# Other prices in the list scheduler of a two-block transformer kernel

## The chip, the cores and the metric

One Trainium2 chip, one of its cores. The time is the device time of one execution in microseconds (us). The kernel before ran three times: 1303.06, 1300.27 and 1302.47 us, median 1302.47. The page and the rows below come from one further look with the hardware profiler.

## The reference

A float32 network on 256 tokens of width 1024, in two blocks; every product has to come out at float32 accuracy. Cut to what matters:

```python
# block 1
h = rmsnorm(x, attn_norm); proj = h @ w_in
o_a = mla_attention(...); o_b = moba_attention(...)          # 8 heads each
x = x + (sigmoid(gate_a) * (o_a @ w_o_mla) + sigmoid(gate_b) * (o_b @ w_o_moba)) @ w_out
x = x + hierarchical_moe(rmsnorm(x, ffn_norm), ...)          # 4 groups of 8 experts, top 2
x = rmsnorm(x, final_norm)
# one expert:  (silu(xb @ w_g[e]) * (xb @ w_u[e])) @ w_d[e]
# block 2, layers l = 0 and 1
x = x + even_mixer(rmsnorm(x), ...)   # l = 0: gated convolution and differential attention
x = x + odd_mixer(rmsnorm(x), ...)    # l = 1: stick-breaking attention
x = x + mem_attention(rmsnorm(x), rmsnorm(mem), ...)
x = x + conv_ffn(rmsnorm(x), w_up, w_conv, w_down)
```

## The kernel before

The activations stay on chip, features on the 128 partitions, the 256 tokens along them. Weights stream in as slabs of 1 MB (128 x 2048 floats), each one DMA of the queue of SyncE (SP). A float32 product is made of three fast ones: a slab `w` is split by ScalarE (ACT) into a rounded part `h` and by VectorE (DVE) into the rest `l`; the activations likewise into `xh` and `xl`; TensorE (PE) then adds xh by h, xl by h and xh by l. In the trace these are the groups of six or so matmuls named `fm` (output by features) and `tm` (output by tokens).

The 32 experts are computed in eight groups of four, g = 0 to 7, each expert on its first 32 tokens. The names of one group, in the order of its data: `ga` gathers the tokens with the selection matrix `st`, which is made from `place`, the token's place in line, itself made from the product `pos`; `cb`, `cs`, `rs` bring the norm factors and the weights of the tokens, from `ct` and `rt`; `gu` are eight products with raw slabs `w_gu`; `act` is the activation, `at` its transposition; `by` are four products with raw slabs `w_dn`, in two banks; `y` copies a bank of `by`; `co` scatters `y` back, and the residual `x` takes it. Expert slabs are used as they are, without `h` and `l`; between the groups steps of the memory's keys and values (slabs `w_xkv`, products `fm` and `tm`, norms `hn_raw`, `hn_sq`, `rsq`, `hn`) are mixed in.

Behind group 1 (LATEG) stands a branch, L1137: tokens that did not fit are computed if there are any, which with these inputs there are not. All engines read a flag and branch. SyncE first waits until its loads have landed.

Nothing of this is issued in the order of the code. The class `Recorder` records every operation with its inputs and outputs; `plan` then plays a list scheduler: each engine has a clock, of the operations that are ready on it the one of the lowest place in the program goes first, its clock moves on by `price`, and what depends on it becomes ready LAG later. Loads keep the order of the program and start as places come free. A place is one buffer of a tag: `w`, `h` and `l` have three each, `n8` six, and a raw expert slab takes a place of whichever of these tags can spare one. When the plan says a place is free depends on the prices, so they also decide which load gets which place, and so for whose last reader it waits. The order that `plan` gives is then issued (`issue`, whose line L461 nearly every instruction shows) and the tile framework adds the semaphores: on the chip each engine runs its list in order, whatever things really take. `barrier` keeps all but loads on their side of the branch.

Of the kernel before, what the change touches and what calls it, by code (L numbers as in the profile page):

```python
# [63 lines left out]
# Each engine runs its instructions in the order in which they are issued. The  # L64
# network is first recorded, phase after phase, on tiles that have no place yet;
# a list scheduler then picks the order, so that an engine that would wait for
# one phase works on the next. Tile places the tiles and makes all waits.
class View:
    """A part of a recorded tile."""
# [54 lines left out]
class Slot:  # L124
    """A recorded tile."""
# [38 lines left out]
class Recorder:  # L164
# [18 lines left out]
    def stray(self, shape, dtype, name):  # L183
        """A tile that takes a place that any of the tags in self.shared can spare."""
        return Slot(self, shape, dtype, name, None, 0, "sb").view()
# [5 lines left out]
    def price(self, engine, method, a, k):  # L191
        n = self.size(a[0])
        if engine == "tensor":
            if method == "transpose":
                return n / 1.2 + 3
            lhs, rhs = a[1], a[2]
            if rhs.dtype == F32R:
                return max(n / 2.4 + 3, 109) if n >= 254 else 213
            if rhs.dtype == BF16:
                return n / 2.4 + 3  # L200
            cost = max(4 * n / 2.4, 400 if n <= 64 else 213) + 3
            m, rows = self.size(lhs), lhs.rows() if isinstance(lhs, View) else lhs.shape[0]
            if m <= 32:
                return cost / 3.5
            return cost / 2 if m <= 64 or rows <= 64 else cost
        if engine == "scalar":
            return 100 + n / 1.2 + (90 if isinstance(k.get("scale"), (View, bass.AP)) else 0) \
                + (90 if "accum_out" in k else 0)
        if engine == "vector":
            src = a[1]  # L210
            if method in ("tensor_copy", "tensor_scalar"):
                psum = isinstance(src, View) and src.tile.space == "ps"
                return 70 + n * (1.04 if psum else 0.52)
            if method == "reciprocal":
                return 70 + 6.4 * n
            if method == "tensor_reduce":
                return 70 + 1.04 * self.size(src)
            return 70 + 1.04 * n + (60 if method == "scalar_tensor_tensor" else 0)
        if engine == "gpsimd":
            return 200 + 3.5 * n  # L220
        return 2915.0 * n / 2048 if engine == "sync" else 100

    def record(self, engine, calls):
# [18 lines left out]
        if engine == "sync":  # L242
            op.lag = 2000.0
# [39 lines left out]
    def barrier(self, fn, views):  # L283
        """All that was recorded before comes before fn(), all that follows after it, except loads."""
# [5 lines left out]
    def plan(self):  # L290
        """An order of everything recorded: on each engine the ready operation of the lowest prio goes first."""
# [17 lines left out]
        def spare(op):  # L309
            """The shared tag that can best spare a place for op: those of earlier ops stay."""  # L310
# [11 lines left out]
        def load():  # L322
            """Start the loads in the order of the program, as far as there are places."""
# [20 lines left out]
        def offer(op):  # L344
            """Hand a free place to each tile that op starts, in the order of the program, if there are."""
# [88 lines left out]
    def run(self):  # L434
# [7 lines left out]
        # a table is loaded as soon as the one before has done its last  # L442
# [21 lines left out]
class Net:  # L464
# [11 lines left out]
    def bank(self, tag, name):  # L476
        """A bank of PSUM: g for products with weights, a and b for chains in turn, m for the rest."""
        return self.rec.tile([128, 512], F32, name, "p" + tag, dict(g=3, a=2, b=2, m=1)[tag], "ps")

    def temp(self, p, name, shape, dt=F32):  # L480
        """A short-lived tile of chain p, or of the norms (p = "s")."""
# [51 lines left out]
    def raw(self, ap):  # L533
        """A slab of weights as it is."""
# [4 lines left out]
    def slab(self, ap, inner, before=None):  # L539
        """A slab of weights in two parts that add up to it exactly, each [128, n / inner, inner].  # L540
        With before, it comes in four pieces, and before(i) comes before piece i."""
# [1142 lines left out]
```

## Time and profile before

| | |
|---|---|
| median of three runs | 1302.47 us (1300.27 to 1303.06) |
| profiled execution, its span | 1302.4 us |
| TensorE, weight loads | 1234.3 us (95%), 1091.3 us (84%) |
| VectorE, ScalarE | 852.8 us (65%), 651.8 us (50%) |
| loads of SyncE's queue | 272.03 MB, 56.1% of 16 DMA engines |
| TensorE's mean granted clock | 0.987 |

The profiled execution is its span; the page gives no other time of it. By stage: block 1's attention to about 235 us, experts 235 to 525, even mixer to about 625, memory attention and first feed-forward to about 900, odd mixer to about 1050, memory attention and second feed-forward to the end. The share of an engine is a mean over these stages; the windows by stretch say more. A busy TensorE need not be at its peak, since the ends of matmuls are modelled.

### The profile page before, as it was taken

The numbers are of one execution on the slowest core, as the hardware profiler recorded it, in microseconds if no ns is written. First come the engines' busy times: TensorE is split into PE (matmuls) and PEld (weight loads), VectorE is DVE, ScalarE is ACT, GpSimd is POOL, SyncE is SP. The second block draws the span as 40 slices with busy tenths as digits, with TensorE's granted clock in tenths as the row PEclk, the third lists the DMA queues.
The fourth block names the chain that finished last, engine by engine and source line by source line (L and its number), as shares of the span: only waits on it lengthen the run. The fifth ranks groups of instructions, "written<-read, shape, count | busy, mean of one in ns | idle before, by whom it ended". The sixth has DMA issues, their size and how long they took to land.

```text
span 1302.4 us, 22667 instructions
## 1 busy us (share of the span) xinstructions
PE 1234.3 (95%) x9325; PEld 1091.3 (84%) x9325; DVE 852.8 (65%) x1529; ACT 651.8 (50%) x1111; POOL 8.9 (1%) x71
## 2 busy tenths in 40 slices
PE   7999999987878876999999999999999999999998
PEld 7988999656545542898999999999998999999997
DVE  7666578524442242898877977777745587877775
ACT  6654455423322231664545655555656655555553
POOL 1000000000000000000000000000000000000000
PEclk9999999998989998999999999999999999999999
DMA  7623375798999989353441555555333251555551
GB/s 257 241 98 130 136 285 204 309 393 333 381 379 396 419 335 406 133 191 123 156 175 66 198 196 186 170 191 193 131 130 114 81 194 66 203 185 189 174 188 65
DMA packets 40143, 273.55 MB, mean 210 GB/s; under 512 B 4576, under 2 KB 4576, under 8 KB 8032
## 3 DMA queue, kind: packets, MB, share of 16 engines
q1 hardware_dynamic: 40032, 272.03, 56.1%
q8 instruction: 75, 1.23, 0.4%
q14 instruction: 36, 0.29, 0.1%
HBM read 270.96 MB, written 1.05 MB: 209 GB/s over the span
## 4 chain that ended last, share of the span: by engine, by line
PE 67%; DVE 4%; DMA 2%; ACT 2%; issue 1%; SPq 0%; DVEq 0%; ACTq 0%
PE fm L461 40%; PE dn L461 10%; PE tm L461 4%; PE gu L461 2%; PE co L461 2%; PE oz L461 2%; DMA w<-w_dn 2%; DVE l L461 2%; PE by L461 2%; PE bo L461 1%; PE mo L461 1%; PE ms L461 1%; PE ga L461 1%; PE hn L461 1%; DMA w<-w_gu 1%
## 5 line engine op out<-in xcount | busy, mean ns | idle before, releaser
L461 PE MATMUL fm<-xh,h 128*128 128x256 f32 x1824 | 529.0, 291 | 14.1 <-ACT h L461 6.6
L461 PE MATMUL fm<-xh,l 128*128 128x256 f32 x1824 | 520.1, 286 | 6.7 <-DVE l L461 6.7
L461 PE MATMUL fm<-xl,h 128*128 128x256 f32 x1824 | 518.5, 285 | 0.0
L461 DVE TENSOR_TENSOR l<-w,h 128x1024 fp32r<-128x1024 f32 (+2 forms) x328 | 383.1, 1191 | 59.9 <-ACT h L461 59.2
L461 ACT ACTIVATE h<-w 128x1024 fp32r<-128x1024 f32 (+2 forms) x328 | 325.4, 1027 | 176.3 <-issue 85.1
L461 PEld LDWEIGHTS fm<-xh,h 128*128 128x128 f32 x1824 | 352.0, 193 | 19.2 <-ACT h L461 7.4
L461 PEld LDWEIGHTS fm<-xh,l 128*128 128x128 f32 x1824 | 352.0, 193 | 8.3 <-DVE l L461 8.0
L461 PEld LDWEIGHTS fm<-xl,h 128*128 128x128 f32 x1824 | 352.4, 193 | 2.1 <-issue 0.7
L461 PE MATMUL tm<-l,xh 128*128 128x256 f32 (+2 forms) x364 | 104.5, 288 | 4.0 <-DVE l L461 4.0
L461 PE MATMUL tm<-h,xh 128*128 128x256 f32 (+2 forms) x364 | 107.2, 296 | 0.1
L461 PE MATMUL tm<-h,xl 128*128 128x256 f32 (+2 forms) x364 | 104.0, 286 | 0.0
L461 DVE SCALAR_TENSOR_TENSOR fc<-fu,partile,fc 128x256 f32<-128x256 f32 x176 | 73.5, 480 | 1.3 <-ACT fc L461 1.3
L461 PEld LDWEIGHTS tm<-l,xh 128*128 128x128 f32 x364 | 69.5, 191 | 5.2 <-DVE l L461 4.6
L461 PEld LDWEIGHTS tm<-h,xh 128*128 128x128 f32 x364 | 69.4, 191 | 3.3 <-issue 1.6
L461 PE MATMUL gu<-w,xs 128*32 128x512 f32 x512 | 65.6, 630 | 6.0 <-DMA w<-w_gu 6.0
L461 PEld LDWEIGHTS tm<-h,xl 128*128 128x128 f32 x364 | 69.5, 191 | 0.4
L461 PE MATMUL dn<-fa,h 128*128 128x256 f32 x352 | 64.2, 282 | 1.1 <-ACT fa L461 0.6
L461 DVE TENSOR_TENSOR x<-x,co 128x512 f32<-128x512 f32 x32 | 21.8, 687 | 57.9 <-PE co L461 57.9
L461 PE MATMUL dn<-h,fa 128*128 128x512 f32 x176 | 57.0, 396 | 0.0
L461 PEld LDWEIGHTS dn<-fa,h 128*128 128x128 f32 x352 | 54.4, 189 | 1.6 <-ACT fa L461 0.8
L461 DVE TENSOR_TENSOR fu<-fm,rbc 128x512 f32<-128x512 f32 x44 | 30.3, 688 | 37.9 <-PE fm L461 37.7
L461 DVE SCALAR_TENSOR_TENSOR act<-gu,rs,act 128x256 f32<-128x256 f32 x8 | 3.9, 484 | 71.8 <-ACT act L461 71.8
(291 smaller groups left out, 1416.1 us busy)
## 6 DMA issues: line engine op xcount, KB each, us to landing
w<-w_gu SPq DMA_DIRECT2D x64, 1024.0 KB, 9.3
w<-w_up SPq DMA_DIRECT2D x44, 1024.0 KB, 4.9
w<-w_dn SPq DMA_DIRECT2D x32, 1024.0 KB, 9.9
w<-w_down SPq DMA_DIRECT2D x22, 1024.0 KB, 4.9
w<-w_xkv SPq DMA_DIRECT2D x16, 1024.0 KB, 8.5
w<-w_in_d SPq DMA_DIRECT2D x8, 1024.0 KB, 4.8
w<-w_xq SPq DMA_DIRECT2D x8, 1024.0 KB, 4.9
w<-w_xo SPq DMA_DIRECT2D x8, 1024.0 KB, 5.1
```

The costliest lines, as they stand in the source:

```text
L461: getattr(getattr(self.nc, op.engine), method)(*map(r, a), **{n: r(v) for n, v in k.items()})
```

## The change

Only the numbers of `price`, and one lag, are others. Where the formulas were the author's, they now follow the durations of a trace: a DMA of a slab 2485 instead of 2915 ns, ready 2400 instead of 2000 later; ScalarE's fixed part 205 instead of 100, VectorE's some 155 instead of 70; a fast matmul of 256 columns 120 instead of 110; transpositions and the slow float32 products by other formulas. Comments and doc strings are gone as well, and an empty line in `price` moves what follows by one line, so L461 is L462 after.

```diff
             if method == "transpose":
-                return n / 1.2 + 3
+                return 109 * max(1.0, n / 128)
             if rhs.dtype == F32R:
-                return max(n / 2.4 + 3, 109) if n >= 254 else 213
+                return max(n / 2.4 + 13.3, 109) if n >= 254 else 213
...
-            cost = max(4 * n / 2.4, 400 if n <= 64 else 213) + 3
+            cost = max(4 * n / 2.4 + 5, 218)
...
         if engine == "scalar":
-            return 100 + n / 1.2 + (90 if isinstance(k.get("scale"), (View, bass.AP)) else 0) \
-                + (90 if "accum_out" in k else 0)
+            return 205 + n / 1.2 + (77 if isinstance(k.get("scale"), (View, bass.AP)) else 0) \
+                + (204 if "accum_out" in k else 0)
...
-                return 70 + n * (1.04 if psum else 0.52)
+                return 155 + n * (1.04 if psum else 0.55)
...
-            return 70 + 1.04 * n + (60 if method == "scalar_tensor_tensor" else 0)
+            return 157 + 1.04 * n + (57 if method == "scalar_tensor_tensor" else 0)
...
-        return 2915.0 * n / 2048 if engine == "sync" else 100
+        return 2485.0 * n / 2048 if engine == "sync" else 100
...
         if engine == "sync":
-            op.lag = 2000.0
+            op.lag = 2400.0
```

Three quarters of TensorE's calls keep their place in its list (the largest move is 120 places), two thirds of VectorE's, 72% of ScalarE's and 257 of SyncE's 278. 26 of the loads get another place: among them the first `w_xkv` slab behind group 2's expert slabs, which had the place that the sixth `gu` of group 2 reads last and now has the second's; the second of these slabs behind group 4's, which had the place of the first `by` and now has that of the last `gu`; and the first `w_gu` slab for group 7, which had a place that frees with `co` and now one that frees with a split `l`.

At the branch, VectorE. What stands ahead of it before, from group 1's activation on:

```order
L461 SCALAR_TENSOR_TENSOR act<-gu,rs,act 128x256
L461 COPY act<-at 128x256
L461 TENSOR_TENSOR x<-x,co 128x512 x4
L461 TENSOR_TENSOR l<-w,h 128x1024 x2
L1127 TENSOR_LOAD flag
L1137 COMPARE_AND_BRANCH
```

And after:

```order
L462 SCALAR_TENSOR_TENSOR act<-gu,rs,act 128x256
L462 COPY act<-at 128x256
L462 TENSOR_TENSOR x<-x,co 128x512 x4
L1128 TENSOR_LOAD flag
L1138 COMPARE_AND_BRANCH
```

The two splits `l` that stood ahead of the branch are gone from there; the same holds on TensorE for 21 `fm`, and on ScalarE for four `h`. What stands on VectorE directly behind the branch (the slow part between, not run, left out), before:

```order
L461 TENSOR_TENSOR hn_raw<-fm,rbm 128x512
L461 TENSOR_TENSOR l<-w,h 128x1024 x2
L461 TENSOR_TENSOR hn_sq<-hn_sq 128x256
L461 TENSOR_TENSOR st<-place,csttile 128x256 x2
L461 TENSOR_TENSOR rsq_t<-rsq_u 128x256
L461 SCALAR_TENSOR_TENSOR rsq_t<-hn,rsq_t 128x256
```

And after:

```order
L462 TENSOR_TENSOR l<-w,h 128x1024 x4
L462 TENSOR_TENSOR hn_raw<-fm,rbm 128x512
L462 TENSOR_TENSOR hn_sq<-hn_sq 128x256
L462 TENSOR_TENSOR st<-place,csttile 128x256 x2
L462 TENSOR_TENSOR rsq_t<-rsq_u 128x256
L462 SCALAR_TENSOR_TENSOR rsq_t<-hn,rsq_t 128x256
```

All four splits are behind the branch now, and all four ahead of `hn_raw`, where before the last two came behind it.

In group 3, TensorE, from the first four `gu` to `co`; four calls make one product with a raw slab. Before:

```order
L461 MATMUL gu<-w,xs 32x512 x16
L461 MATMUL hn<-hn_sq,ones 128x256
L461 MATMUL gu<-w,xs 32x512 x4
L461 MATMUL cb<-csttile,ct 128x128
L461 MATMUL gu<-w,xs 32x512 x4
L461 MATMUL cb<-csttile,ct 128x128 x3
L461 MATMUL rs<-ones,rt 128x1 x4
L461 MATMUL gu<-w,xs 32x512 x8
L461 MATMUL at<-csttile,act 128x128 x2
L461 MATMUL by_6731<-w,act 32x512 x4
L461 MATMUL by_6736<-w,act 32x512 x4
```

And after:

```order
L462 MATMUL gu<-w,xs 32x512 x16
L462 MATMUL hn<-hn_sq,ones 128x256
L462 MATMUL gu<-w,xs 32x512 x16
L462 MATMUL at<-csttile,act 128x128 x2
L462 MATMUL cb<-csttile,ct 128x128
L462 MATMUL by_6721<-w,act 32x512 x4
L462 MATMUL cb<-csttile,ct 128x128 x3
L462 MATMUL rs<-ones,rt 128x1 x4
L462 MATMUL by_6732<-w,act 32x512 x4
L462 MATMUL by_6721<-w,act 32x512 x4
L462 MATMUL co<-cs,y 128x256 x4
```

`cb` and `rs` stood between the `gu`; now all eight `gu` and `at` come first, and `cb` and `rs` stand among `by`.

In the even mixer, VectorE, around the first `cu` (the convolution's gated input; `nm` the maxima of the scores, `eqk` queries and keys). Before:

```order
L461 TENSOR_REDUCE nm<-sc 128x1 x3
L461 TENSOR_SCALAR nm<-nm 128x2
L461 TENSOR_REDUCE nm<-sc 128x1
L461 TENSOR_TENSOR cr<-fm,rr 128x256
L461 TENSOR_SCALAR nm<-nm 128x2
L461 TENSOR_TENSOR xl<-sl_y,xh 128x256
L461 TENSOR_TENSOR cu<-fm,cr 128x256
L461 TENSOR_TENSOR cy<-fm,rbc_7902 128x256
L461 RECIPROCAL sm<-sm 128x2
L461 TENSOR_TENSOR l<-w,h 128x1024
```

And after:

```order
L462 SCALAR_TENSOR_TENSOR eqk<-hn_raw,partile,rsq_u 128x256 x2
L462 TENSOR_TENSOR l<-w,h 128x1024 x2
L462 TENSOR_REDUCE nm<-sc 128x1
L462 TENSOR_TENSOR rsq_t<-rsq_u 128x256
L462 TENSOR_REDUCE nm<-sc 128x1
L462 SCALAR_TENSOR_TENSOR rsq_t<-sl,rsq_t 128x256
L462 TENSOR_SCALAR nm<-nm 128x2
L462 TENSOR_REDUCE nm<-sc 128x1
L462 TENSOR_SCALAR rsq_t<-rsq_t 128x256
L462 TENSOR_REDUCE nm<-sc 128x1
L462 TENSOR_TENSOR rsq_u<-rsq_u,rsq_t 128x256
L462 RECIPROCAL sm<-sm 128x2
```

The two splits that stood here singly behind `cu` now come as a pair directly behind `eqk`, ahead of the maxima.

## Rows read from the trace of the kernel before

**Rows 1.** The page's first line.

```profile
span 1302.4 us, 22667 instructions
```

**Rows 2.** Windows of 50 us: width, busy time (and count) by engine, PEclk, DMA share, GB/s.

```profile
250.00:300.00 50.00, 41.09 (x309) 24.92 (x300) 13.95 (x18) 12.90 (x18) 0.00 (x0) 1.00 0.92 373
...
450.00:500.00 50.00, 40.42 (x311) 27.20 (x310) 22.56 (x41) 16.86 (x24) 0.00 (x0) 1.00 0.92 355
...
550.00:600.00 50.00, 49.99 (x391) 45.91 (x390) 47.89 (x107) 31.46 (x64) 0.00 (x0) 1.00 0.46 162
...
750.00:800.00 50.00, 50.00 (x419) 50.00 (x418) 38.27 (x61) 25.69 (x42) 0.62 (x6) 1.00 0.55 194
```

**Rows 3.** The transfers of the expert stage, 235 to 525 us.

```profile
DMA packets 15082, 110.05 MB, mean 379 GB/s; under 512 B 1664, under 2 KB 1664, under 8 KB 1664
```

**Rows 4.** Windows by stretch inside the expert stage, columns as in rows 2.

```profile
291.00:296.00 5.00, 3.32 (x23) 2.98 (x22) 3.65 (x4) 2.94 (x4) 0.00 (x0) 1.00 0.28 66
...
301.00:307.00 6.00, 5.90 (x29) 5.93 (x29) 0.00 (x0) 0.00 (x0) 0.00 (x0) 0.53 1.00 406
...
307.00:317.00 10.00, 8.32 (x68) 8.06 (x67) 6.31 (x12) 4.72 (x6) 0.00 (x0) 1.00 0.76 270
...
325.00:336.00 11.00, 7.69 (x66) 2.52 (x58) 2.70 (x7) 2.32 (x3) 0.00 (x0) 1.00 0.78 305
336.00:370.00 34.00, 27.76 (x192) 19.48 (x196) 19.86 (x40) 11.93 (x21) 0.00 (x0) 0.92 1.01 420
370.00:384.00 14.00, 10.92 (x69) 5.08 (x62) 3.56 (x6) 3.56 (x5) 0.00 (x0) 0.95 0.87 323
...
402.00:412.00 10.00, 8.04 (x51) 4.10 (x51) 2.47 (x4) 3.08 (x5) 0.00 (x0) 1.00 0.88 344
...
480.00:492.00 12.00, 9.60 (x63) 7.79 (x64) 8.38 (x10) 6.28 (x7) 0.00 (x0) 1.00 0.70 241
```

**Rows 5.** The branch's line: operation, ns min/median/max, first and last start in us.

```profile
L1137 ACTq COMPARE_BRANCH  x1: 50/50/50, 290.9 to 290.9; - x1
L1137 DVEq COMPARE_BRANCH  x1: 72/72/72, 293.4 to 293.4; - x1
L1137 ACTq EVENT_SEMAPHORE  x1: 17/17/17, 294.0 to 294.0; - x1
L1137 PEldq COMPARE_BRANCH  x1: 5972/5972/5972, 295.0 to 295.0; - x1
L1137 DVEq EVENT_SEMAPHORE  x1: 21/21/21, 297.0 to 297.0; - x1
```

**Rows 6.** The chain of waits behind the branch: start us, us, what.

```profile
301.10 5.94 PE fm L461 x27
...
307.67 1.23 DVE l L461
...
308.94 2.90 PE fm L461 x22
```

**Rows 7.** The timeline of SyncE's queue, 309.5 to 311 us: start us, us, operation.

```profile
310.05 1.79 SPq L461 DMA_DIRECT2D w<-w_gu  x2
```

**Rows 8.** TensorE's waits: line, waited for, us in total, times, longest.

```profile
PE fm L461 <- PEq L1137: 4.4, 1, 4.4
...
PE cb L461 <- DVE ct L461: 3.0, 1, 3.0
...
PE fm L461 <- DVE cu L461: 2.4, 2, 2.1
```

**Rows 9.** The timeline of VectorE behind group 6, [idle before <- releaser] at the end.

```profile
486.29 6.89 DVE L461 TENSOR_TENSOR l<-w,h 128x1024 fp32r<-128x1024 f32 x6
```

**Rows 10.** The timeline of VectorE in the routing.

```profile
237.41 0.22 DVE L461 SCALAR_TENSOR_TENSOR place<-pos,sel 128x64 f32<-128x64 f32 x1 [1.77 <-PE pos L461]
...
237.69 0.41 DVE L461 TENSOR_TENSOR st<-place,csttile 128x256 fp32r<-128x256 f32 x1
```

**Rows 11.** The timeline of VectorE in the even mixer.

```profile
609.71 0.42 DVE L461 TENSOR_TENSOR cu<-fm,cr 128x256 f32<-128x256 f32 x1
...
610.44 1.21 DVE L461 TENSOR_TENSOR l<-w,h 128x1024 fp32r<-128x1024 f32 x1
```

More of the change, by code (lines that the diff above doesn't have):

```diff
@@ L194, in price @@
             if method == "transpose":
-                return n / 1.2 + 3
+                return 109 * max(1.0, n / 128)
             lhs, rhs = a[1], a[2]
             if rhs.dtype == F32R:
-                return max(n / 2.4 + 3, 109) if n >= 254 else 213
+                return max(n / 2.4 + 13.3, 109) if n >= 254 else 213
             if rhs.dtype == BF16:
                 return n / 2.4 + 3
-            cost = max(4 * n / 2.4, 400 if n <= 64 else 213) + 3
+            cost = max(4 * n / 2.4 + 5, 218)
             m, rows = self.size(lhs), lhs.rows() if isinstance(lhs, View) else lhs.shape[0]
             if m <= 32:
-                return cost / 3.5
-            return cost / 2 if m <= 64 or rows <= 64 else cost
+                return cost / 4
+            return cost / 2 + 50 if m <= 64 or rows <= 64 else cost
         if engine == "scalar":
-            return 100 + n / 1.2 + (90 if isinstance(k.get("scale"), (View, bass.AP)) else 0) \
-                + (90 if "accum_out" in k else 0)
+            return 205 + n / 1.2 + (77 if isinstance(k.get("scale"), (View, bass.AP)) else 0) \
+                + (204 if "accum_out" in k else 0)
         if engine == "vector":
@@ L212, in price @@
                 psum = isinstance(src, View) and src.tile.space == "ps"
-                return 70 + n * (1.04 if psum else 0.52)
+                return 155 + n * (1.04 if psum else 0.55)
             if method == "reciprocal":
-                return 70 + 6.4 * n
+                return 155 + 6.4 * n
             if method == "tensor_reduce":
-                return 70 + 1.04 * self.size(src)
-            return 70 + 1.04 * n + (60 if method == "scalar_tensor_tensor" else 0)
+                return 150 + 1.04 * self.size(src)
+            return 157 + 1.04 * n + (57 if method == "scalar_tensor_tensor" else 0)
         if engine == "gpsimd":
             return 200 + 3.5 * n
-        return 2915.0 * n / 2048 if engine == "sync" else 100
+        return 2485.0 * n / 2048 if engine == "sync" else 100
     def record(self, engine, calls):
```

## The prediction

> **What bounds the kernel now.** I read the page first, then the windows of 50 us, then the transfers of the expert stage, and last the stretches in which the transfers pause. The span is 1302.4 us [rows 1]. It is not one bound but three. In the feed-forward stretches TensorE and its weight loads are both busy 50.00 of 50 us: nothing that an order can give back. In the expert stage, about 235 to 525 us, TensorE has 8.9 us idle in 250-300 and 9.6 in 450-500, while the DMA engines are 92% busy. In 550-600 VectorE is busy 47.89 of 50 beside a full TensorE [rows 2]. So the expert stage is where time can be won, and the even mixer is where it can be lost.
>
> The expert stage moves 110.05 MB in 290 us, a mean of 379 GB/s [rows 3]. Where nothing holds it up it runs at 420 (336-370 us) [rows 4]. At that pace the bytes need 262 us, so 28 us are pauses. The reader is to see in rows 4 that they lie in a few places. What each costs is (420 - its rate) / 420 x its width:
> - 291-296: 66 GB/s, 4.2 us. SyncE drains its loads ahead of the branch.
> - 307-317: 270 GB/s, 3.6 us.
> - 325-336: 305 GB/s, 3.0 us.
> - 370-384: 323 GB/s, 3.2 us.
> - 402-412: 344 GB/s, 1.8 us.
> - 480-492: 241 GB/s, 5.1 us.
>
> That is 20.9 of the 28. Each is a load that waited for a place whose last reader came late. A price list that moves those readers moves the loads, and as every load behind queues in order, a pause that goes is won for the whole rest of the stage.
>
> The Trainium skill (DMA: Bandwidth & Descriptors, section Bandwidth) says that a core's transfers from memory bind at about 358 GB/s, and gives 435 as the ceiling of the ports. By 358 the 110.05 MB would need 307 us, more than they took, so there would be nothing to win here and the sum would be about zero or above. The 420 of rows 4 contradict it, and the measurement decides.
>
> **The change, part by part.** No instruction is added or removed; only the order, and with it the places, differ. Six places matter.
>
> *The branch (-3.6).* Before, TensorE issues 21 fm matmuls ahead of the branch and VectorE two of the four splits `l`. TensorE's branch takes 5.97 us, VectorE's holds it from 293.4 to 297.0 (3.6 us), ScalarE's is over at 294.0 [rows 5]. TensorE then runs 27 fm at 0.22 us each (5.94), because its granted clock is 0.53 of full, the lower level, after the idle time [rows 4, 6]. Only after them does VectorE get to hn_raw and the last two splits, since they stand behind hn_raw in its queue; the last one ends at 310.0, and only then the next load is issued, at 310.05 [rows 6, 7]. That is the pause of 307-317. After the change VectorE's order has all four splits directly behind the branch and ahead of hn_raw. VectorE leaves the branch at about 296.5 to 297, four splits at 1.23 end at about 301.5, and the load can go 8 us earlier, while the four loads ahead of it are still landing. So this pause closes fully: -3.6. The other side: TensorE meets its branch with nothing queued, at about 291 instead of 295, and is out at about 297; the 48 fm, 27 at 0.22 and 21 at 0.13, end at about 306, against 307.04 before. What is late next is fm itself, whose ends free the next places, and it is not later. SyncE issues one load more ahead of its drain, which shifts the drain by one load and leaves its 4.2 us.
>
> The Trainium skill (Runtime: NRT & Kernel Launch, section Instruction fetch mechanics) says that a taken branch whose target lies outside the fetched window stalls its engine while the page is fetched. The 5.97 us agree with such a stall. By that rule the matmuls queued ahead of the branch were free cover, and going in with an empty queue exposes 1.5 us more (4.4 idle before [rows 8], 5.97 after); if the path ran through TensorE there, the gain would be 2.1 and not 3.6. The rows put the path through VectorE's splits, so I keep 3.6.
>
> *Group 2, 325-336 (-3.0).* The first loads of the next slab take the place that the second gu product frees, where before it was the sixth's, three to four products later, behind the wait for rs. Also by's last product goes ahead of co, and two splits `l` ahead of the updates of x. The load is issued before the queue is empty, so the pause closes.
>
> *Group 3, 370-384 (-3.2).* Before, cb stands between the gu products and waits 3.0 us for ct [rows 8], and rs behind it; two gu and all of by come after. After, all gu go first, then at, and cb and rs stand among by. The places of those two gu come free earlier by that wait, 3.0 us, and by the length of cb and rs: together at least the pause. The cover for cb's wait is then the gu products; if ct is still late, by waits instead, and its places are freed late: it costs up to 3.0 again.
>
> *Group 4, 402-412 (-1.8).* No reader moves much; the load there took the place of the first by product and now takes that of the last gu. With 10 us won by then on TensorE's side and less on the loads', by can start as its loads land. I take it whole, and 0 as the other end.
>
> *Pause 480-492 (+1.0).* Same order on TensorE, but the first load now takes the place of the second of six splits in a row (6.89 us for six, so 2.3 us after 486.3) instead of co's [rows 9]. The load after the next moves the other way. Landing in order, one of the two lost is caught up: +1.0, between 0 and 2.9.
>
> *Start, routing and the even mixer (+3.7).* At the start a piece of a slab (0.26 MB, 0.6 us at 420 GB/s) goes ahead of a piece of x that the first products need: +0.6, 0 to 0.6. In the routing, pos goes behind seven groups of tm, directly ahead of the gathers ga, which need st: from place at 237.41 to the end of st at 238.10 [rows 10] nothing covers it any more: +0.7. In the even mixer VectorE is the bound. Two splits of 1.21 us that came behind cu now stand ahead of the maxima `nm` and cu [rows 11], and fm already waits for cu, 2.4 us in all [rows 8]: +2.4. The bounds are wide. Between pt and the next scores six fm groups of six matmuls stood as filler (36 x 0.13 = 4.7 us) and now none: with no cover up to +4.7 more. Below, the splits are done sooner, so the fm after them wait less: -2.4. I take +2.4, the row that is nearest.
>
> The attention before 235 us is reordered too, more fill between the steps of the chains, but TensorE shows hardly an idle microsecond there: 0, from -3 to +2. Behind 725 us nearly every row stands where it stood.
>
> Sum: -3.6 - 3.0 - 3.2 - 1.8 + 1.0 + 0.6 + 0.7 + 2.4 = -6.9. The profiled execution's span was 1302.4 and the median of the runs 1302.47, so they stand for one another: 1302.4 - 6.9 = **1295.5 us**.
>
> **The rivals.**
> - *Everything arrives, and nothing is lost in the mixer.* -11.6 in the four pauses, the mixer 0, the attention -3, the rest +1.3 + 1.0: about 1290. For it: DMA is at its pace right behind every pause, so nothing else holds it. Against it: the mixer's VectorE is full.
> - *The pauses only move.* A place that comes free earlier fills one load, but the next reader is on the same chain of gu, at, by, co, and the queue runs dry one group later. Then only the branch's 3.6 stays, and start, routing, 480-492 and the mixer give back 4.7: 1303.5, with the mixer at half its price 1302.3. For it: TensorE is busy 41 of 50 us in the stage, so it has no great reserve to stay ahead. Against it: between the pauses loads run at 420 for 34 us on end.
> - *The mixer decides; slower.* VectorE there has 2 us free in 50. Four splits (4.8 us) are pulled ahead of the chain of maxima, and the 4.7 us of fill are used up before the chain needs them: 9.5 us on a path that alternates between VectorE and TensorE, and the fm after the wait run at the lower clock. With half of the pauses' gain (-5.8) and the 2.3 of the small terms: 1308.4. It decides once the gain in the expert stage is under about 9. For it: fm already waits there. Against it: the total of VectorE's work is the same, and what is pulled ahead is missing behind.
> - *That the new prices order nothing differently* is out: the branch, group 3 and the mixer stand otherwise, and only then time can move.
>
> **How the numbers follow.** Differences under 0.2%, 2.6 us, can't be told from none here. Forecast 0.50; everything arrives 0.13; pauses only move 0.20; the mixer decides 0.17. Faster by over 0.2% (below 1299.9): 0.63. Within: 0.20. Slower (above 1305.1): 0.17. The range: its low end takes the four pauses whole with the low ends of the mixer and the attention (1302.4 - 11.6 - 2.4 - 3 + 1 = 1286.4); its high end takes in the pauses that only move, 1303.5, and stops at 1305, leaving out most of the slower case. On its own the forecast reaches from 1290 to 1300.
>
> **What would show it right or wrong.** Right: in the windows of the profile after, no stretch of 10 us at 270 GB/s behind the branch, the two splits done by about 302, no wait of cb for ct, and the last bytes of the experts some 8 us earlier; the feed-forward unchanged. The mixer's term: the wait of fm for cu grows to about 5. Wrong: the same sum of pauses at other places; a new wait of by for ct; TensorE idle at the mixer's scores; or a shift already in the attention, of which I count nothing.

## The result, and the profile after

The kernel after takes 1309.3 us (median of 5 runs, 1308.2 to 1312.1), the kernel before beside it 1302.9; the recorded ratio is 1.0059, with a 95% interval of 1.0042 to 1.0076 (a recorded ratio can differ by some 0.1% from the quotient of two medians, here 1.0049). The kernel after is slower by some 0.5%, where 1295.5 us was forecast. The profiled execution's span is 1307.5 us.

The stretches of [rows 4] in the profile after (width, busy time and count of TensorE, its weight loads, VectorE, ScalarE and GpSimd, granted clock, share of the DMA engines, GB/s):

```profile
301.00:307.00 6.00, 4.82 (x22) 4.54 (x23) 4.63 (x4) 2.11 (x3) 0.00 (x0) 0.51 0.95 348
307.00:317.00 10.00, 10.00 (x81) 9.95 (x79) 2.44 (x6) 4.09 (x5) 0.00 (x0) 0.95 1.02 424
325.00:336.00 11.00, 8.69 (x78) 3.04 (x74) 4.05 (x12) 2.66 (x4) 0.00 (x0) 1.00 0.96 375
336.00:370.00 34.00, 30.30 (x234) 19.52 (x226) 20.61 (x42) 13.35 (x23) 0.00 (x0) 1.00 0.96 383
370.00:384.00 14.00, 12.43 (x84) 10.43 (x85) 5.41 (x7) 3.48 (x6) 0.00 (x0) 1.00 1.01 421
...
402.00:412.00 10.00, 7.67 (x49) 5.84 (x48) 6.91 (x8) 4.49 (x5) 0.00 (x0) 1.00 1.01 419
412.00:480.00 68.00, 57.03 (x418) 36.68 (x416) 17.15 (x33) 16.34 (x25) 0.00 (x0) 0.92 0.96 383
480.00:492.00 12.00, 9.38 (x60) 7.57 (x61) 8.09 (x9) 6.45 (x8) 0.00 (x0) 1.00 0.43 149
```

Of the four pauses of the forecast three are closed and the second is half closed: 424 instead of 270 GB/s, 375 instead of 305, 421 instead of 323, 419 instead of 344. But 336-370, which ran at 420 before, now runs at 383; 480-492 fell from 241 to 149; and 412-480, at 383 here, ran at 408 before:

```profile
412.00:480.00 68.00, 55.97 (x444) 37.44 (x442) 21.85 (x38) 18.41 (x28) 0.00 (x0) 1.00 1.00 408
```

TensorE's waits after (line, waited for, us in total, times, longest), to be held against [rows 8]:

```profile
PE gu L462 <- DMA w<-w_gu: 7.9, 8, 1.4
...
PE fm L462 <- DVE cu L462: 4.4, 2, 3.9
PE fm L462 <- PEq L1138: 4.0, 1, 4.0
...
PE by L462 <- DMA w<-w_dn: 3.1, 3, 1.3
```

The 3.0 us of `cb` for `ct` are gone, as forecast. The wait for `cu` has grown from 2.4 to 4.4. The 4.0 behind the branch stand against 4.4.

To see where time went, both traces were matched call by call. A number behind # counts the operations in the order of the code ("op" in the expectations). The table gives, for six stretches between two of TensorE's matmuls, how many us longer (+) the stretch was than in the profiled execution before. Its heads are the times before: 31-162 is the attention, 229-244 the routing up to the last `ga` of group 0 (op 1217), 244-383 the experts up to `co` of group 3 (op 1603), 383-459 up to op 1867, 459-531 the rest of the experts (op 2062), 537-660 the even mixer. The runs under it are the experiments below; medians are of their timed runs, without two of no_sync that took over twice the usual time, and the ratio is to the kernel before on the same chip.

| kernel | median | ratio, 95% interval | 31-162 | 229-244 | 244-383 | 383-459 | 459-531 | 537-660 |
|---|---|---|---|---|---|---|---|---|
| after | 1309.3 | 1.0059 [1.0042, 1.0076] | +1.6 | +1.4 | -10.7 | +6.3 | +0.3 | +6.0 |
| att_new | 1303.1 | 1.0008 [0.9985, 1.0031] | +1.6 | -0.1 | -2.9 | +1.3 | -3.2 | -1.5 |
| mix_old | 1307.3 | 1.0034 [1.0017, 1.0051] | +1.6 | +1.3 | -10.7 | +6.5 | -0.4 | +4.8 |
| mix_new | 1311.7 | 1.0061 [1.0040, 1.0081] | 0.0 | 0.0 | -1.2 | +1.5 | -2.0 | +7.8 |
| moe_new | 1304.4 | 1.0018 [1.0000, 1.0036] | 0.0 | +1.5 | -11.1 | +3.9 | +0.4 | +4.7 |
| conv_new | 1312.4 | 1.0078 [1.0055, 1.0100] | +1.6 | +1.4 | -10.7 | +6.3 | +0.4 | +9.2 |
| conv_moe_new | 1302.2 | 0.9997 [0.9981, 1.0012] | 0.0 | +1.5 | -10.9 | +3.0 | -1.0 | +1.6 |
| conv_old | 1307.1 | 1.0043 [1.0023, 1.0063] | 0.0 | 0.0 | +0.5 | -0.2 | -2.1 | +3.5 |
| place148 | 1307.5 | 1.0048 [1.0030, 1.0066] | +1.6 | +1.3 | -10.9 | +6.5 | -0.4 | +6.4 |
| cin_new | 1298.9 | 0.9963 [0.9947, 0.9978] | +1.6 | +1.5 | -9.5 | +5.9 | -0.4 | -2.6 |
| cin_moe_new | 1296.2 | 0.9940 [0.9917, 0.9963] | 0.0 | +1.4 | -9.1 | +6.1 | -0.5 | -4.2 |
| mix_va | 1308.3 | 1.0051 [1.0034, 1.0068] | +1.6 | +1.4 | -10.3 | +5.0 | +0.5 | +6.0 |
| mix_pe | 1300.9 | 0.9986 [0.9969, 1.0004] | +1.6 | +1.4 | -11.2 | +6.2 | -0.3 | -1.5 |
| cin_old | 1297.6 | 0.9952 [0.9933, 0.9971] | 0.0 | -0.1 | +1.0 | +1.4 | -1.3 | -4.9 |
| moe_sync | 1305.3 | 1.0025 [1.0014, 1.0037] | 0.0 | 0.0 | -2.7 | 0.0 | +0.5 | +4.6 |
| moe_rest | 1292.7 | 0.9925 [0.9909, 0.9941] | 0.0 | +1.5 | -6.6 | -0.5 | -2.0 | -2.3 |
| no_sync | 1304.0 | 1.0018 [1.0000, 1.0037] | +1.6 | +1.4 | -9.6 | +1.5 | +1.0 | +5.1 |
| two_out | 1297.7 | 0.9967 [0.9950, 0.9984] | +1.6 | +1.4 | -7.0 | -0.3 | -1.0 | -1.1 |
| best | 1290.3 | 0.9919 [0.9892, 0.9945] | 0.0 | +1.3 | -10.5 | +3.5 | -1.8 | -4.3 |

Where a stretch has the order of before (244-531 in att_new, mix_new, conv_old and cin_old), the table also shows what a repeat gives: together -4.8, -1.7, -1.8 and +1.1 us. The nine kernels whose traces have after's order in the experts (after, mix_old, moe_new, conv_new, conv_moe_new, cin_new, cin_moe_new, mix_va and mix_pe) have together -3.5 to -8.9 us there, median -4.6. Repeats of one order thus lie some 5 us apart: a difference of a few us in the experts can't be read from one trace, and the stretch 459-531 of the profiled execution before was itself some 2 us slow. In the mixer repeats lie closer: after, place148 and no_sync, which have one order there, +6.0, +6.4 and +5.1.

In the kernel after, 10.7 us are won up to 383 us, 6.6 are lost again in the rest of the experts, 3.0 in the attention and the routing and 6.0 in the mixer. With 0.5 at the start and little outside these stretches that makes the 5.1 us between the two spans.

### The profile page after: what moved, and what is told of

Read it like the earlier page. It is cut to its first block, busy times and chain, and to the rows that moved or that the text cites. A ratio compares the mean times of both kernels' runs of the same rounds, so it can differ in the third digit from the quotient of the medians.

```text
span 1307.5 us, 22672 instructions
## 1 busy us (share of the span) xinstructions
PE 1236.7 (95%) x9325; PEld 1091.8 (84%) x9325; DVE 852.5 (65%) x1529; ACT 651.0 (50%) x1111; POOL 7.4 (1%) x71
## 4 chain that ended last, share of the span: by engine, by line
PE 67%; DVE 4%; DMA 3%; ACT 2%; issue 1%; SPq 0%; DVEq 0%; ACTq 0%
PE fm L462 41%; PE dn L462 10%; PE tm L462 4%; PE oz L462 2%; DVE l L462 2%; PE gu L462 2%; DMA w<-w_gu 2%; PE co L462 2%; PE by L462 1%; DMA w<-w_dn 1%; PE bo L462 1%; PE ms L462 1%; PE mo L462 1%; PE ga L462 1%; PE hn L462 1%
## 5 line engine op out<-in xcount | busy, mean ns | idle before, releaser
L462 PE MATMUL fm<-xh,h 128*128 128x256 f32 x1824 | 531.5, 292 | 17.1 <-ACT h L462 6.7
L462 PE MATMUL fm<-xh,l 128*128 128x256 f32 x1824 | 519.6, 285 | 2.9 <-DVE l L462 2.9
L462 PE MATMUL fm<-xl,h 128*128 128x256 f32 x1824 | 519.5, 285 | 0.0
L462 DVE TENSOR_TENSOR l<-w,h 128x1024 fp32r<-128x1024 f32 (+2 forms) x328 | 382.9, 1191 | 68.6 <-ACT h L462 64.2
L462 ACT ACTIVATE h<-w 128x1024 fp32r<-128x1024 f32 (+2 forms) x328 | 325.7, 1027 | 201.5 <-issue 86.4
L462 PEld LDWEIGHTS fm<-xh,h 128*128 128x128 f32 x1824 | 352.8, 194 | 23.5 <-ACT h L462 13.6
L462 PEld LDWEIGHTS fm<-xh,l 128*128 128x128 f32 x1824 | 352.6, 193 | 3.8 <-DVE l L462 3.6
L462 PEld LDWEIGHTS fm<-xl,h 128*128 128x128 f32 x1824 | 352.9, 194 | 2.3 <-issue 0.7
L462 PE MATMUL tm<-l,xh 128*128 128x256 f32 (+2 forms) x364 | 104.3, 287 | 3.2 <-DVE l L462 3.2
L462 PE MATMUL tm<-h,xh 128*128 128x256 f32 (+2 forms) x364 | 106.9, 295 | 0.0
L462 PE MATMUL tm<-h,xl 128*128 128x256 f32 (+2 forms) x364 | 103.8, 286 | 0.0
L462 DVE SCALAR_TENSOR_TENSOR fc<-fu,partile,fc 128x256 f32<-128x256 f32 x176 | 73.6, 479 | 1.3 <-ACT fc L462 1.3
L462 PEld LDWEIGHTS tm<-l,xh 128*128 128x128 f32 x364 | 69.6, 191 | 4.4 <-DVE l L462 3.6
L462 PE MATMUL gu<-w,xs 128*32 128x512 f32 x512 | 64.8, 620 | 8.1 <-DMA w<-w_gu 7.9
L462 PEld LDWEIGHTS tm<-h,xh 128*128 128x128 f32 x364 | 69.5, 191 | 2.1 <-issue 1.4
L462 PEld LDWEIGHTS tm<-h,xl 128*128 128x128 f32 x364 | 69.5, 191 | 0.3
L462 PE MATMUL dn<-fa,h 128*128 128x256 f32 x352 | 64.2, 282 | 1.1 <-ACT fa L462 0.6
L462 DVE TENSOR_TENSOR x<-x,co 128x512 f32<-128x512 f32 x32 | 21.8, 686 | 55.9 <-PE co L462 55.9
L462 PE MATMUL dn<-h,fa 128*128 128x512 f32 x176 | 57.0, 396 | 0.0
L462 PEld LDWEIGHTS dn<-fa,h 128*128 128x128 f32 x352 | 54.4, 189 | 1.6 <-ACT fa L462 0.8
L462 DVE TENSOR_TENSOR fu<-fm,rbc 128x512 f32<-128x512 f32 x44 | 30.2, 687 | 38.9 <-PE fm L462 38.9
L462 PEld LDWEIGHTS gu<-w,xs 128*32 128x32 f32 x512 | 14.6, 111 | 43.8 <-issue 24.6
```

The costliest lines, as they stand in the source:

```text
L462: getattr(getattr(self.nc, op.engine), method)(*map(r, a), **{n: r(v) for n, v in k.items()})
```

## The experiments

In all of them both price lists are in the kernel, and a switch says, for four parts of the program, on which engines the new one counts: attention; experts with routing; norms and even mixer; the rest.

```diff
+SEL = ALL, ALL, ALL, ALL
...
     def price(self, engine, method, a, k):
+        return (self.price_new if engine in self.sel else self.price_old)(engine, method, a, k)
```

### One part of the program at a time

```diff
+SEL = ALL, ALL, NONE, ALL     # mix_old
+SEL = NONE, NONE, ALL, NONE   # mix_new
+SEL = NONE, ALL, NONE, NONE   # moe_new
+SEL = ALL, NONE, NONE, NONE   # att_new
```

mix_old: 

> The new prices everywhere, but the old ones for all that the norms between the blocks and the even mixer record. Theory 1 (the even mixer's own order costs about 6 us: in the traces the new kernel is 0.7 us ahead at 537 us and 5.6 behind at 640): 1303 us, 1301 to 1305, and TensorE through with the mixer 0 to 2 us behind the kernel before. Theory 2 (the mixer is late because of what the expert stage hands over, loads and places and filler that it used up): the mixer stays 5 us behind and the time is 1307 or more.

mix_new: 

> The old prices everywhere, but the new ones for the norms between the blocks and the even mixer. Theory 1: the mixer's order alone costs about 6 us, 1308.5 us, 1306 to 1310, with a wait of fm for cu of 3 to 4 us. Theory 2: within 2 us of the kernel before, since attention and experts are as they were.

moe_new: 

> The old prices everywhere, but the new ones for the expert stage with its routing. Theory 1 (by the traces the expert stage of the new kernel wins about 4 us from 243 to 537 us): 1298.5 us, 1296 to 1301, the pause of the transfers behind the branch gone. Theory 2 (the 4 us are only the clock's and the queue's mood at the end of the stage, and what is won goes back at the pause of 480 to 492 us): 1301 to 1304.

att_new: 

> The old prices everywhere, but the new ones for block 1's attention, gates and output. Theory 1 (by the traces the new kernel is 2.0 us behind at 205 us, lost between 60 and 160 us): 1304.5 us, 1303.5 to 1306. Theory 2 (a loss there is absorbed, since the expert stage is bound by its transfers): 1302 to 1303.

The mixer with its own new prices loses 7.8 us (mix_new). But with its old prices it loses 4.8 and 4.7 as well, once the experts ahead of it have the new ones (mix_old, moe_new). Old prices don't bring the old order back: the two have one and the same order in the mixer, and it is not that of before, since `plan` comes there with other clocks and places. So the theory that the mixer's own prices lose the time was only half right: the two ways don't add up (after has +6.0), and something in the mixer turns each of these orders into a loss. The attention's +1.6 came back with its prices alone and made no difference that the timed runs can tell.

### The places of the convolution's temps

The timeline of VectorE after, in the mixer (start us, us, operation, [idle before <- releaser]):

```profile
611.79 0.42 DVE L462 TENSOR_TENSOR rsq_u<-rsq_u,rsq_t 128x256 f32<-128x256 f32 x1
...
612.27 0.48 DVE L462 SCALAR_TENSOR_TENSOR sl_y<-bo,partile,rsq_u 128x256 f32<-128x256 f32 x1
612.67 0.41 DVE L462 TENSOR_TENSOR cr<-fm,rr 128x256 f32<-128x256 f32 x1
613.00 0.41 DVE L462 TENSOR_TENSOR cy<-fm,rbc 128x256 f32<-128x256 f32 x1
613.33 0.41 DVE L462 TENSOR_TENSOR cu<-fm,cr 128x256 f32<-128x256 f32 x1
```

`cr` needs only the `fm` that TensorE had done at 590 us, and VectorE is never idle for over 0.4 us from 591 on, yet `cr` comes at 612.67, right behind `sl_y`, the end of head 2's chain. Both take one of the four places of the tag `ta`, which are handed out in the order of the code. `cu` frees the PSUM bank that the next `fm` needs: that is its 3.9 us wait. TensorE has no other `fm` left to cover it:

```profile
605.00 0.74 PE L462 MATMUL pt<-csttile,p 128*128 128x128 f32 x3 [0.81 <-DVE p L462]
606.48 0.89 PE L462 MATMUL bo<-pt,ev 128*128 128x256 f32 x4 [0.74 <-DVE pt L462]
...
609.41 0.50 PE L462 MATMUL sc<-ali,bf 128*128 128x128 bf16 x4
613.79 0.58 PE L462 MATMUL fm<-xh,h 128*128 128x256 f32 x1 [3.88 <-DVE cu L462]
```

conv_new, conv_moe_new and conv_old move `cr` and `cu` to the two places of `ts`, idle in the mixer; place148 tests the pause at 480-492 instead.

```diff
-                cr = self.temp(p, "cr", [128, T])
-                u = self.temp(p, "cu", [128, T + 2])
+                cr = self.temp("s", "cr", [128, T])
+                u = self.temp("s", "cu", [128, T + 2])
```

```diff
-            for tag in self.shared:
+            for tag in ("n8",) if op.idx == 2014 else self.shared:   # place148
```

conv_new: 

> The changed kernel, with the temps cr and cu of the mixer's convolution put into the two temp places of tag ts, which stand idle in the mixer, and no longer behind the temps of heads 2 and 3 in ta and tb. Theory (the mixer loses because cr#2500 can start only once head 2 has given its temp places back, while its products stood ready some 15 us, and fm#2550 waits for the PSUM bank that cu#2501 frees): the wait of fm on cu (3.9 us at its longest, after) goes, and the stretch of the mixer gives back 4 to 6 us of the 6.0 us lost; whole kernel 1303 to 1305. Rival (filler products ahead of bo, hn and pt on TensorE's queue, and VectorE idle 3.5 us at 587 us, are the loss by themselves): the wait goes but the mixer stays 4 us or more behind, 1307 to 1309.5.

conv_moe_new: 

> New prices in the expert stage and the routing alone, old prices elsewhere, and cr and cu in the places of tag ts. The same kernel without the move of cr and cu took 1304.4 (ratio 1.0018) and lost 4.7 us in the mixer. Theory (the place): the 5.7 us wait of fm on cu goes, the expert stage's 3 us stay, 1297 to 1300, faster than before. Rival (the filler order): no change from 1304.

conv_old: 

> All old prices, and cr and cu in the places of tag ts. Before waits 2.4 us of fm on cu. Theory (the place): it gains those 2 us, at most 3 (1300 to 1301); so the place costs before less than it costs the changed order. Rival (the place matters to no order): 1302.5 to 1303.

place148: 

> The changed kernel, with the load of op 2014 (load 148) put into a place of the 4 KB tag n8, as in before, where the changed scheduler had put it into a place of tag w that comes free later. Theory (the longer pause at 482 to 493 us is from that place): the gap ahead of load 148 falls from 6.8 to about 2.4 us, the stream is some 4 us earlier at 494 us, and the second half of the stage gains 2 to 4 us: 1305.5 to 1307.5. Rival (TensorE there waits for more than the stream, so the pause is hidden): the gap goes and the time stays, 1309.

conv_new, conv_old and place148 came out as neither theory said. TensorE's waits in conv_new's mixer:

```profile
PE fm L500 <- DVE cu L500: 5.7, 1, 5.7
PE fm L500 <- DVE cy L500: 4.5, 1, 4.5
```

The wait had only moved, to the next block's `cu`, which now stood behind two places instead of four, and to `cy`, still in `ta`. conv_old is slower than before too (1307.1, mixer +3.5), with a wait of 6.3 us for `cy` where before waits 2.4 for `cu`. Only conv_moe_new gained (mixer +1.6 instead of +4.7). In place148 the gap ahead of the load stayed at 6.6 us, as the place of `n8` that it was given was also read last by a split; the idea was not tested by it, and its 1307.5 says nothing on it.

### The convolution in place, and the mixer's prices by engine

cin_new and cin_moe_new compute `cr`, `cu`, `cv` and `cy` of a block in one tile of `ts`, so that no part of it waits for a place of the heads.

```diff
-                cr = self.temp(p, "cr", [128, T])
-                u = self.temp(p, "cu", [128, T + 2])
+                cx = self.temp("s", "cx", [128, 2 * T + 2])
+                cr, u = cx[:, 0:T], cx[:, T:2 * T + 2]
...
-                o = self.temp(p, "cv", [128, T])
-                self.conv(o, u, w)
-                us.append(o)
+                self.conv(cr, u, w)
+                us.append((cr, u[:, 0:T]))
...
-                y = self.temp("ab"[n], "cy", [128, T])
+                o, y = us[n]
...
+SEL = ALL, ALL, ALL, ALL                        # cin_new
+SEL = NONE, ALL, NONE, NONE                     # cin_moe_new
+SEL = ALL, ALL, ("vector", "scalar"), ALL       # mix_va, convolution as in after
+SEL = ALL, ALL, ("tensor", "sync"), ALL         # mix_pe, convolution as in after
```

cin_new: 

> The changed kernel, with the whole convolution (cr, cu, cv and cy) in one temp of tag ts for each of its four column blocks, computed in place, so that none of it waits for a place of the heads' temps. In conv_new the wait for places had only moved, to cu of the next block (5.7 us) and cy (4.5 us). Theory (places): no wait of fm on cu or cy over 1 us is left and the mixer's 123.4 us of before come back within 2 us (after +6.0, conv_new +9.2): whole kernel 1303.5 to 1306. Rival (products moved ahead of head 0's and head 1's transposes are the loss: all of it lies before 607 us, +4.8 to +5.7): mixer +4 to +6 as in after, 1308 to 1310.

cin_moe_new: 

> New prices in the expert stage and the routing alone, old ones elsewhere, and the convolution in place in ts. conv_moe_new: mixer +1.6 us, one wait of 4.5 us on cy, 1302.2. Theory (places): that wait goes, mixer -1 to 0, expert stage -5 to -9: 1298 to 1301, faster than before by 0.1 to 0.35%. Rival (TensorE was not on the path at that wait, since its other products fill): 1302 as conv_moe_new.

mix_va: 

> The changed kernel, with the new prices of VectorE and ScalarE in the norms and the even mixer, and there the old ones of TensorE. Theory (a dearer VectorE makes the scheduler think that head 0's scores and transposes come late, so it places filler products ahead of them): mixer +4 to +6 with the loss before 607 us, as in after; 1308 to 1309.5. Rival (the dearer short products and transposes of TensorE do it): mixer about +4.8 with the loss behind 607 us, as in mix_old; 1306 to 1307.5.

mix_pe: 

> The other half: in the norms and the even mixer the new prices of TensorE and the old ones of VectorE and ScalarE. Theory (VectorE's prices move the filler): no loss before 607 us (-1 to +1 there), the rest of the loss behind it as in mix_old; 1306 to 1307.5. Rival (TensorE's prices): +4 to +5 us by 607 us; 1308 to 1309.5.

TensorE's waits in the mixer, of cin_new, then of mix_va, then of mix_pe:

```profile
PE fm L500 <- ACT xh L500: 0.6, 1, 0.6
PE fm L500 <- DVE l L500: 0.5, 1, 0.5
```

```profile
PE fm L500 <- DVE cu L500: 5.3, 2, 4.1
PE sc L500 <- DVE eqk L500: 1.8, 2, 1.3
```

```profile
PE fm L500 <- DVE cu L500: 0.7, 1, 0.7
PE sl L500 <- ACT sl_sq L500: 0.6, 1, 0.6
```

With the convolution out of the heads' places no wait for `cu` or `cy` is left and the mixer's +6.0 becomes -2.6, all else of the change in place (the order in the mixer changes with the places). Of the mixer's new prices it is VectorE's and ScalarE's that lose (mix_va +6.0); without them it is -1.5. mix_pe keeps the places, and `cr` comes right behind `sl_y` there too, but at 604.07, and `fm` that wait for nothing stand as cover behind the scores, which end at 602.4:

```profile
603.68 0.48 DVE L500 SCALAR_TENSOR_TENSOR sl_y<-bo,partile,rsq_u 128x256 f32<-128x256 f32 x1
604.07 0.41 DVE L500 TENSOR_TENSOR cr<-fm,rr 128x256 f32<-128x256 f32 x1
```

So the shared place costs time where the order leaves no cover. Over all 20 kernels the wait goes with the loss: where `fm` waits in the mixer at most 1.4 us for `cu` and `cy` together, the mixer has -1.1 to -4.9; before and att_new, with 2.4 us, have 0 and -1.5; all others, with 4.4 us and more, have +1.6 to +9.2.

### The places under the old prices, and the experts' prices by engine

```diff
+SEL = NONE, NONE, NONE, NONE                           # cin_old, convolution in place
+SEL = NONE, ("sync",), NONE, NONE                      # moe_sync
+SEL = NONE, ("tensor", "vector", "scalar"), NONE, NONE # moe_rest
```

cin_old: 

> All old prices, and the convolution in place in tag ts as in cin_new and cin_moe_new. Theory (the places and the new prices act together: under the old prices fm waits 2.4 us for cu in all): mixer -1 to -3 us, whole kernel 1300 to 1301.5, so the places account for about 2 us by themselves and for 10 us (after to cin_new) under the new prices. Rival (the places cost both orders the same): mixer -8 us, 1294 to 1296, and the new prices are slower by 3 us or more with the convolution in place too.

moe_sync: 

> New price and lag of the loads alone (2485 ns per 2048 columns instead of 2915, lag 2400 instead of 2000), in the expert stage and the routing alone; all else old. Against the four runs with the old order the stretch from op 1217 to op 1603 gains 9.8 us under all new prices. Theory (the scheduler's dearer loads had it believe that places would be waited for less, so the places that the loads get, and the pauses, hang on the loads' price): 1217 to 1603 -7 to -11. Rival (the engines' prices decide which work frees a place first): 0 to -3. In both the gain is given back by op 1867, since the stream behind has no gap: 1301 to 1304.

moe_rest: 

> The other half: new prices of TensorE, VectorE and ScalarE in the expert stage and the routing, the loads' price and lag old, all else old. Theory (the loads' price moves the pauses): 1217 to 1603 0 to -3 us, routing +1.4 us as in after; 1302 to 1304.5. Rival (the engines' prices): 1217 to 1603 -7 to -11 us, given back by op 1867 as in after.

The places cost the old order 4.6 us too (1302.2 to 1297.6), more than expected; under the new prices they cost 10.4 (1309.3 to 1298.9, on two chips). By the recorded ratios it is some 6 and 12. With the convolution in place the mixer differs by 2.3 us between the price lists, -4.9 and -2.6.

The loads' price was expected to close the pauses; the engines' prices close more of them (-6.6 against -2.7), and keep the gain: from 244 to 531 us moe_rest wins 9.1 us (-6.6 - 0.5 - 2.0), moe_sync 2.2. This is one trace of each, but the four kernels without the loads' new price (moe_rest, and below no_sync, two_out and best) have one order in the experts and win 7.1 to 9.1 there, against a median of 4.6 for after's order and of 1.7 for before's own. SyncE's longest waits from 470 to 500 us, in moe_sync and in moe_rest:

```profile
SPq L500 <- DVE l L500: 12.2, 3, 9.0
```

```profile
SPq L500 <- DVE l L500: 6.3, 3, 2.5
...
SPq L500 <- PE co L500: 6.0, 1, 6.0
```

The 9.0 us wait for a split `l`, which makes the longer pause at 480-492, comes with the loads' new price alone. And moe_sync's mixer, whose own prices are old, loses 4.6 us: that the experts ahead of it are planned otherwise is enough, since its order is then another than before's.

### The two prices taken out of the change

```diff
+SEL = (("tensor", "vector", "scalar"),) * 4                          # no_sync
+SEL = (_E := ("tensor", "vector", "scalar")), _E, ("tensor",), _E    # two_out
+SEL = NONE, ("tensor", "vector", "scalar"), NONE, NONE               # best, convolution in place
```

no_sync: 

> The change without its loads' part: new prices of TensorE, VectorE and ScalarE everywhere, price and lag of the loads as before. The order in the mixer is that of the changed kernel. Theory (two prices lose, by themselves and in different stages: the loads' some 5 us in the expert stage, VectorE's and ScalarE's 6 to 8 us in the mixer): expert stage -8 to -10 us, routing +1.4, attention +1.6, mixer +5 to +6.5; 1302 to 1304. Rival (the loads' price is the one cause, and the mixer's loss is what it hands over, as moe_sync's 4.6 us suggest): mixer -2 to 0 and 1293 to 1296.

two_out: 

> The change without the loads' part, and in the norms and the even mixer with the old prices of VectorE and ScalarE; all its other new prices stand. Theory (these two are what loses): expert stage -8 to -10 us, routing +1.4, attention +1.6, mixer -1 to -3; 1293 to 1296.5. Rival (the order in the mixer loses with TensorE's prices too where the loads' are old): mixer +2 or more, 1298 or more.

best: 

> The order of moe_rest (new prices of TensorE, VectorE and ScalarE in the expert stage and the routing alone) with the convolution in place in tag ts. Theory (the places still cost this order the 1.4 us that fm waits for cu, and some clock): mixer -4 to -5 us instead of -2.3, 1290 to 1292. Rival (nothing left to gain there): 1292.7 as moe_rest.

no_sync keeps 7.1 us at the end of the experts (-9.6 + 1.5 + 1.0), where after keeps 4.1, and loses 5.1 in the mixer: 1304.0. Without VectorE's and ScalarE's new prices in the mixer as well, two_out takes 1297.7, faster than before. So two of the new prices lose, some 5 us (1309.3 to 1304.0) and 6 us (1304.0 to 1297.7), and the rest of the change gains. VectorE's and ScalarE's lose in the mixer itself. Where the loads' price loses differs: moe_new has it and moe_rest doesn't, and of the 11.7 us between their medians the traces have 2.3 in the experts and 7.0 in the mixer, whose prices are old in both. The best kernel tried takes 1290.3; its interval overlaps with that of moe_rest. In its mixer TensorE is full (width, busy time, clock, DMA share, GB/s):

```profile
523.00:650.00 127.00, 126.73 (x1014) 1.00 0.45 158
```

## Why the prediction was wrong

**The step that failed first** is the sentence that a pause that goes "is won for the whole rest of the stage". The pauses were read rightly, and up to 383 us TensorE won 10.7 us. Of the stream itself less was won. Its shift at single loads, the landing after less the landing before, was +2.0 us as the stage began (load 69); 0.0 behind the branch (load 84), since the loads ahead had been up to 3.7 late; +1.5 at load 104; -1.5 at load 109; -3.7 at loads 122 to 136. That is 5.7 of the 11.6. At 383 us TensorE was 7.3 us ahead of its old time on a stream that was 1.5 ahead. The windows over 383-459, before and then after (TensorE alone: width, busy, clock, DMA share, GB/s):

```profile
384.00:460.00 76.00, 63.65 (x495) 1.00 0.99 410
```

```profile
376.00:458.00 82.00, 69.06 (x501) 0.96 1.01 413
```

The DMA engines have nothing left in either, so TensorE's lead had to shrink to the stream's 3.7: that is 3.6 of the +6.3. The other 2.7 fit the clock, though no run set it. Of the 6 us that the window after is longer, 5.4 are busy time for the same calls, at a granted clock of 0.96, and only 0.6 idle time; the waits for `w_dn` loads grew from 1.3 to 3.1 us. moe_new has the same order in the experts and got the full clock in this stretch:

```profile
373.00:453.00 80.00, 66.58 (x502) 1.00 1.01 419
```

It lost 3.9 us there, and TensorE ended as far ahead as the loads were, 6.1 us. That the full stream sets this time is read from these traces; no run took it away. It is in part the rival "the pauses only move", with more of the gain kept than that rival said.

By the forecast's terms: the experts gave -4.1 instead of -10.6 us, the mixer cost 6.0 instead of 2.4, and the routing and the attention 3.0 instead of 0.7.

Then the pieces, one by one:
- *Branch.* As forecast VectorE does all four splits behind the branch, and 307-317 runs at 424. It left the branch at 301.2, not at 297:

```profile
L1138 PEldq COMPARE_BRANCH  x1: 5103/5103/5103, 295.5 to 295.5; - x1
L1138 DVEq COMPARE_BRANCH  x1: 72/72/72, 297.5 to 297.5; - x1
...
L1138 DVEq EVENT_SEMAPHORE  x1: 21/21/21, 301.2 to 301.2; - x1
```

  The pause's 3.6 us were won, and part of them lost ahead of it: of the 3.6 the stream kept 2.0. The forecast had TensorE at its branch at about 291 with nothing queued; it came at 295.5, with `co` still running to 296.9. So the queue was not empty, and the 1.5 us more did not come: 4.0 waited against 4.4.
- *Group 2.* (375 - 305) / 420 x 11 = 1.8 of the 3.0 won, and (420 - 383) / 420 x 34 = 3.0 lost right behind. There the pause did move: SyncE's longest wait for a split `l` from 334 to 347 us is 5.3 us, where before it is 2.5 (after, then before):

```profile
SPq L462 <- DVE l L462: 8.5, 2, 5.3
```

```profile
SPq L461 <- DVE l L461: 2.5, 1, 2.5
```

- *Groups 3 and 4.* Right in mechanism and size: no wait of `cb`, and 421 and 419 GB/s.
- *Pause 480-492.* +1.0 was forecast. At 149 instead of 241 GB/s it is (241 - 149) / 420 x 12 = 2.6. The place changed as described, and the load was issued with the end of the second of the six splits, at 488.95, where before it went at 485.71 (the timelines of SyncE's queue and of VectorE):

```profile
488.95 6.61 SPq L462 DMA_DIRECT2D w<-w_gu  x7
```

```profile
486.57 6.89 DVE L462 TENSOR_TENSOR l<-w,h 128x1024 fp32r<-128x1024 f32 x6
```

  Only 1.2 us were caught up two loads later, so the term was mis-sized, inside its bounds: the stream went from +0.2 at load 146 to +3.7 at load 149 and +2.5 behind it. The lead of 3.7 that it had at load 136 was lost before this pause: TensorE was no longer ahead, and load 143, which waited for a place that its `gu` frees, went out at 467.6 us, before at 467.3.
- *Start, routing, attention.* The start's +0.6 is within what repeats show. The routing lost 1.4 instead of 0.7, in every run with the engines' new prices there: `place` now waits 4.28 us for `pos`, against 1.77 in [rows 10]:

```profile
241.98 0.23 DVE L462 SCALAR_TENSOR_TENSOR place<-pos,sel 128x64 f32<-128x64 f32 x1 [4.28 <-PE pos L462]
```

  The attention lost 1.6, where 0 was taken, inside its bounds.
- *The mixer, mis-sized*: +2.4 was taken, +6.0 came; the upper bound, 7.1, held it. The sign that the forecast named, a wait of about 5 for `cu`, came as 4.4. What it had as the bound alone, that the six groups of `fm` behind `pt` are used up, is what the trace shows: no `fm` from 604.2 to 613.8. What it didn't have is the place of `cr`, which ties `cu` to the end of head 2 (cin_new). The two splits in front stand in that chain and delay it too; no run took them out alone. Behind the wait the clock is lower as well, 0.74 in 607-620 against 0.87 before.

By size the nearest rival was "the mixer decides; slower" with 1308.4: more than half of the gain was lost, and VectorE's and ScalarE's new prices lose in the mixer by themselves (mix_va). That its number is so near is partly luck: it took 9.5 us for the mixer, where 6.0 came, and nothing for the attention. It had too small a chance, since the sum took each stage's gain for certain to reach the end.

## What to carry to other kernels

A pause of a full load stream is won only if the stream is earlier at the next load and every load behind it: count the shift of the landings from load to load, not the pauses, and hold TensorE's lead against it. Truer prices for a list scheduler need not give a better order: try them engine by engine and stage by stage, since here the same list held a gain of 7 to 9 us in the experts and losses of 5 and 6. Where a reordering loses at one wait, look for the place that the waiting operation shares with an unrelated chain; freeing it was worth 4.6 us under the old list and 10.4 under the new.

## What the runs showed that was not expected

The same order does not get the same clock each time. The experts' last 11 us before, and the same stretch in mix_new, whose order there is that of before (TensorE alone: width, busy, granted clock, DMA share, GB/s):

```profile
520.00:531.00 11.00, 10.00 (x45) 0.77 0.55 229
```

```profile
517.30:528.30 11.00, 8.69 (x53) 1.00 0.84 348
```

At 0.77 a part of the stretch ran at the lower of the two levels, 1.2 GHz. Four kernels with before's order in the experts took 1.3 to 3.2 us less from 459 to 531 us than the profiled execution before; that this one trace is a slow sample there could not be seen from it alone.
